# Two linear-attention directions paired on the PE array, and background modulation steps moved forward

## The chip, the cores and the metric

The kernel runs on one core of one Trainium2 chip. The time is device microseconds of one execution, from launch to the last result; the figure given for a kernel is the median of several executions. Engines are named as in the profile: PE is TensorE (matmuls), PEld its weight loads, DVE is VectorE, ACT is ScalarE, POOL is GpSimd, SP is SyncE, which here issues nearly all DMAs.

## The reference, cut to what matters

Two blocks of two layers each run over 256 latent tokens and 256 context tokens of width 1024, all in float32. The first block's layers compute windowed attention, a Fourier mix and a short convolution, gated and merged. Every layer is modulated: shift, scale and gate come from a small vector times a 1024 x 3072 matrix.

```python
def layer(x, ctx, c, c_ctx, w_mod, b_mod, ...):
    shift, scale, gate = jnp.split(jax.nn.silu(c) @ w_mod + b_mod, 3, axis=-1)
    hx = rmsnorm(x, g_pre) * (1 + scale[:, None]) + shift[:, None]
    ...
    x_new = x + gate[:, None] * rmsnorm(y, g_post)
```

The second block has nine modulation vectors per layer (`ada_w`), feed-forward stages, one even mixer and one odd mixer. The odd mixer is a gated linear attention with four heads, in chunks of 64 tokens, run forwards and backwards; the two results are added:

```python
def step(smat, inp):                       # one chunk of one direction
    ...
    o = a @ vc + qe @ smat                 # output of this chunk
    kd = kc * jnp.exp(bl - bcum)
    smat = jnp.exp(bl)[..., None] * smat + kd.T @ vc      # state for the next
    return smat, o
yx = yx_f + jnp.flip(yx_b, axis=1)
```

## The kernel before, in words

Weights come as chunks of 256 columns (1 MB) through `wload`, are split by ACT and DVE into a high and a low half (`wchunk`, L183 and L184), and each projection takes three one-pass products per 128 x 128 tile (`mm3`, L193 to L195). A raw chunk lies in one of three buffers during the first block: two of the pool `wraw` (tag `wr`) and one of `rx` (tag `xr`), handed out in turn. The split halves have two buffers each. A scheduler orders each engine's instructions at build time, by priority in program order and by a model of times; where a helper `row` is used, its products are issued one after the other in the order given.

**First block.** `fb_layer` runs for layer 0 and layer 1. While its projections run, a `hook` after each column tile of 128 does one step of the windowed attention and then `self.bg(HB)`: `HB` = 1 step from the queue `self.bgq` of background generators, taken in order. A generator that is at its end is dropped and the next one gives the step. Layer 0 has 16 such hooks. The queue holds `bga` (the modulation columns 2048 to 3072 of layer 0, 4 steps), `bgb` (the modulation of layer 1, 12 steps), `load_T` of the second block's context (3 steps: two with eight transposes each, L543, and copies, L545; one with the squares and sums of a norm's statistics) and `bgc` (modulation columns 0 to 3072 of the second block, 12 steps). A modulation step (`mods_pe`) loads 1 MB through the same `wload` (L319) and multiplies it (L322). `load_T` takes its raw tile from `wraw` and holds it until its second step. Its statistics (`Stat`) hold one buffer of tag `sq` (of three) and one of tag `sqa` (of two) until `c2stat.finish()` late in layer 1. After the hooks of layer 0 comes `drain_until(bgb)`, which steps the queue until `bgb` has left it. Then come the output projection (`twice`, six chunk loads), residual and norm, and layer 1, whose column tiles also do steps.

**Odd mixer.** A `plan` says which parts of the linear attention run in which hook of the value and gate projections. `begin` makes the state from the context, `advance(h, step)` does one chunk of both directions of head `h`: direction 0 takes chunk `step`, direction 1 chunk `3 - step`, so that they always use opposite halves of 64 rows. For each direction in turn it issues the output product (L1646: all 128 rows, 64 columns, into one half of the partitions), takes a bank `wk` of PSUM (the pool has three), issues the state product (L1649: 64 rows, 128 columns) and lets DVE update the state (L1651). The last of the four steps has no state product. Hooks 7, 8, 13 and 14 of the plan advance two heads with state products one after the other.

Of the kernel before, what the change touches and what calls it, by code (L numbers as in the profile page):

```python
# [10 lines left out]
ALU = mybir.AluOpType  # L11
# [34 lines left out]
C2A = 0  # L46
# [12 lines left out]
HB = 1  # L59
# [63 lines left out]
class Kern:  # L123
# [428 lines left out]
    def first_block(self):  # L552
        nc, I, tc = self.nc, self.I, self.tc
        V = self.vseg
        st = [self.Stat(self), self.Stat(self)]
        self.rope_tables(self.cp)
        with self.rawpool(RI):
            for _ in self.load_T(I["x"][0], self.X, st[0], self.wload):
                pass
            for i, _ in enumerate(self.mods_pe(I["w_mod"][0, :, 0:2048], 2048, self.m1[0][:, :, 0:16], V["bmod"][:, 0:16],  # L560
                                               self.cst, PM)):
                if i == 0:
                    self.late[0]()
                elif i == 3:
                    rbx = st[0].finish(alloc=self.sc)
                elif i == RL:
                    self.late[1]()
        st[0] = rbx
        bga = self.mods_pe(I["w_mod"][0, :, 2048:3072], 1024, self.m1[0][:, :, 16:24], V["bmod"][:, 16:24], self.cst)
        bgb = self.mods_pe(I["w_mod"][1], 3072, self.m1[1], V["bmod"][:, 24:48], self.cst)  # L570

        def ada():
            cst = self.set_cst(32)
            yield from self.mods_pe(I["ada_w_2"][0, :, 0:3072], 3072, self.m2[0][:, :, 0:24], V["adab0"][:, 0:24], cst)
        bgc = ada()
        self.c2stat = self.Stat(self)
        self.bgq = [bga, bgb, self.load_T(I["ctx_2"][0], self.C2, self.c2stat, act=C2A), bgc]
        with self.rawpool(RB), tc.tile_pool(name="fb", bufs=1, reuse_waits="tile") as self.fb:
            self.fb_layer(0, st, bga, bgb, self.fb_AB(0))
            if self.dbg != "fb0":  # L580
                self.fb_layer(1, self.nstat, None, bgc, self.nextAB)

# [6 lines left out]
    def fb_layer(self, l, stats, bga, bgb, AB):  # L589
        nc, I, tc = self.nc, self.I, self.tc  # L590
# [65 lines left out]
        def q_proj(c, korder=False, hook=None):  # L656
            self.proj(headchunk(0, c), c01, xn, qsegs, lambda i, ps: ev_q(i, ps, c), korder=korder, hook=hook, alloc=None if upd else self.facc)
# [57 lines left out]
        def attend():  # L715
            last = None
            for t in range(4):
                pso = None
                for si in range(nseg):
                    for i in range(2):  # L720
                        E = scores(t, si, i)
                        if last is not None:
                            values(*last)
                        if pso is None:
                            pso = self.wk()
                        last = (t, si, i, E, pso)
                        yield
            values(*last)
            yield

        att_gen = attend()

        def hook():
            next(att_gen, None)
            self.bg(HB)

        gf = [f1(f"gf{t}", TW) for t in range(2)]
        uf = [f1(f"uf{t}", TW) for t in range(2)]
# [55 lines left out]
        if l == 0:  # L794
# [4 lines left out]
            pss = [[self.facc() for _ in c01] for _ in first]  # L799
            for v, seg in enumerate(SEGS):  # L800
                if v == 1:
                    self.norm_seg(1, stats[1], A, B, PX)
                for j, ch in enumerate(first):
                    for i, cf in enumerate(c01):
# [3 lines left out]
                        if v == 1:  # L808
                            (ev_q if j else ev_kv)(i, pss[j][i])
            self.late[2]()  # L810
            q_proj(1, hook=hook)
        else:

# [8 lines left out]
            fourier()  # L822
            self.proj(self.wcols(w, 512), c01, xn, SEGS, ev_kv, hook=bgs(LB[3]))
            hook()
            self.proj(self.wcols(w, 2304), c01, xn, qsegs, ev_cc, hook=hook)
        if l == 0:
# [14 lines left out]
        h = self.xn  # L841
# [639 lines left out]
    def odd_mixer(self, stats):  # L1481
        nc, I, tc = self.nc, self.I, self.tc
# [6 lines left out]
        mm = nc.tensor.matmul  # L1489
        with self.rawpool(RO), tc.tile_pool(name="od", bufs=1, reuse_waits="tile") as od:  # L1490
# [9 lines left out]
            vt = od.tile([P, 4, D], F32, name="vt")  # L1500
# [3 lines left out]
            kT, qT, gs, kds, ats = {}, {}, {}, {}, {}  # L1504
# [122 lines left out]
            S, po, osbs = {}, {}, {}  # L1627
            vh = lambda h: slice(h * 256, (h + 1) * 256)
# [11 lines left out]
                    mm(po[h][i], ats[h][:, i], vt[:, i, vh(h)], start=(i == 0), stop=False)  # L1640

            def advance(h, step):
                for d in range(2):
                    c = 3 - step if d else step
                    i, r = c // 2, slice(64 * (c % 2), 64 * (c % 2) + 64)
                    mm(po[h][i][r], gs[h, d][0][:, c * 64:(c + 1) * 64], S[h, d], start=False, stop=(step == 3))  # L1646
                    if step < 3:
                        ps = self.wk()
                        mm(ps[:, 0:256], kds[h, d][r, i], vt[r, i, vh(h)], start=True, stop=True)  # L1649
                        s2 = od.tile([P, 256], F32, name="S", tag="S", bufs=6)  # L1650
                        nc.vector.scalar_tensor_tensor(s2, S[h, d], gs[h, d][4][:, c:c + 1], ps[:, 0:256], ALU.mult, ALU.add)  # L1651
                        S[h, d] = s2

            def norm(h):
# [12 lines left out]
            def gate(h):  # L1667
# [15 lines left out]
                4: [(turn, 1), (gates, 2)],  # L1683
                5: [(begin, 0, self.sc), (intra, 1), (decays, 2)],
                6: [(advance, 0, 0), (turn, 2), (begin, 1, self.sc), (gates, 3)],
                7: [(advance, 0, 1), (advance, 1, 0), (intra, 2), (decays, 3)],
                8: [(advance, 0, 2), (advance, 1, 1), (turn, 3)],
                9: [(advance, 0, 3), (advance, 1, 2), (intra, 3)],
                10: [(norm, 0), (advance, 1, 3)],
# [70 lines left out]
```

## Time and profile before

| | |
|---|---|
| median of 3 runs | 2285.04 us (2280.15 to 2288.1) |
| profiled execution | 2283.41 us |
| its span, first to last instruction | 2281.2 us |
| PE busy | 2207.0 us (97%) |
| DVE busy | 1540.7 us (68%) |
| ACT busy | 891.0 us (39%) |
| DMA | 327.27 MB, mean 143 GB/s |

Matmuls are pipelined, so "busy" counts from start to modelled end and overlaps between neighbours; the pace is read from one start to the next. A note such as `[2.07 <-ACT wh L177]` at the end of a row says that the engine was idle 2.07 us before it, and which instruction released it.

### The profile page before, as it was taken

To read this page: it belongs to the slowest core of one execution; us is meant where nothing else is said; L and a number is where in the kernel's file an instruction comes from. 1 tells how busy PE (TensorE), PEld (TensorE's weight loads), DVE (VectorE), ACT (ScalarE), POOL (GpSimd) and SP (SyncE) were. 2 spreads that over 40 slices of the span, in tenths; PEclk is the share of its full clock that TensorE was granted. 3 is DMA by queue.
4 is the path that set the end of the run, shared out by engine and by line. 5 is a ranking of instruction groups with operands and counts; after the bars stand their busy time and mean duration, and the time that the engine had idled before them with its cause. 6 is when DMAs were issued, how large, how long until landed. Compare 5 with 4: busy or idle time off the path is not lost.

```text
span 2281.2 us, 33404 instructions
## 1 busy us (share of the span) xinstructions
PE 2207.0 (97%) x13271; PEld 1882.1 (83%) x13271; DVE 1540.7 (68%) x3348; ACT 891.0 (39%) x1645; POOL 50.0 (2%) x113
## 2 busy tenths in 40 slices
PE   6999889999999999999999999999999999998998
PEld 4777786898888899877988888898888897778998
DVE  4644577786999876667769833469769475556555
ACT  3533555653222245444432221342222245534444
POOL 1000000000000000000000000000000010000000
PEclk8999999999999999999999999999999999999999
DMA  8334445644566432112436423245557242124553
GB/s 301 130 135 155 132 144 208 189 160 160 194 207 203 139 115 93 56 38 75 135 98 217 154 87 111 83 153 185 166 178 255 93 139 75 56 85 144 183 183 129
DMA packets 299179, 327.27 MB, mean 143 GB/s; under 512 B 9260, under 2 KB 290916, under 8 KB 295952
## 3 DMA queue, kind: packets, MB, share of 16 engines
q1 hardware_dynamic: 295968, 321.16, 43.7%
q8 instruction: 104, 1.70, 0.3%
q10 hardware_dynamic: 1952, 2.29, 0.3%
q0 software_dynamic: 1104, 1.70, 0.2%
q14 instruction: 51, 0.42, 0.1%
HBM read 324.07 MB, written 1.05 MB: 143 GB/s over the span
## 4 chain that ended last, share of the span: by engine, by line
PE 49%; issue 41%; DVE 5%; ACT 2%; DMA 2%; POOL 1%; SPq 0%; POOLq 0%; DVEq 0%; ACTq 0%
PE acc L193 9%; PE acc L194 9%; PE acc L195 9%; PE sc L193 3%; PE sc L194 3%; PE sc L195 3%; DVE wl L184 2%; PE acc L322 1%; PE acc L1090 1%; PE acc L1092 1%; PE acc L1091 1%; PE wk L704 1%; PE sc L1401 1%; ACT wh L183 1%; PE wk L1344 1%
## 5 line engine op out<-in xcount | busy, mean ns | idle before, releaser
L193 PE MATMUL acc<-xh,wh 128*128 128x256 f32 (+1 forms) x1792 | 611.5, 343 | 11.2 <-DVE qs L654 5.2
L195 PE MATMUL acc<-xh,wl 128*128 128x256 f32 (+1 forms) x1792 | 606.7, 339 | 5.9 <-DVE wl L184 5.9
L194 PE MATMUL acc<-xl,wh 128*128 128x256 f32 (+1 forms) x1792 | 606.8, 339 | 1.8 <-DVE xl L426 1.7
L183 ACT CAST wh<-wr 128x1024 fp32r<-128x1024 f32 (+1 forms) x394 | 385.9, 1024 | 542.6 <-PE acc L194 256.0
L184 DVE TENSOR_TENSOR wl<-wr,wh 128x1024 fp32r<-128x1024 f32 (+1 forms) x394 | 454.7, 1190 | 162.4 <-ACT wh L183 160.4
L193 PEld LDWEIGHTS acc<-xh,wh 128*128 128x128 f32 x1792 | 342.2, 192 | 69.7 <-issue 24.3
L195 PEld LDWEIGHTS acc<-xh,wl 128*128 128x128 f32 x1792 | 342.8, 191 | 42.8 <-DVE wl L184 6.5
L194 PEld LDWEIGHTS acc<-xl,wh 128*128 128x128 f32 x1792 | 343.2, 192 | 40.7 <-issue 5.0
L293 DVE SCALAR_TENSOR_TENSOR macc<-mraw,vec,macc 128x256 f32<-128x256 f32 x728 | 309.2, 477 | 2.4
L193 PE MATMUL sc<-xh,wh 128*128 128x256 f32 (+1 forms) x816 | 271.4, 333 | 6.3 <-ACT xh L425 3.5
L194 PE MATMUL sc<-xl,wh 128*128 128x256 f32 (+1 forms) x816 | 270.2, 332 | 0.9 <-DVE xl L426 0.9
L195 PE MATMUL sc<-xh,wl 128*128 128x256 f32 (+1 forms) x816 | 270.7, 332 | 0.0
L193 PEld LDWEIGHTS sc<-xh,wh 128*128 128x128 f32 x816 | 155.5, 191 | 22.0 <-ACT xh L425 4.4
L194 PEld LDWEIGHTS sc<-xl,wh 128*128 128x128 f32 x816 | 155.1, 190 | 15.4 <-DVE xl L426 1.3
L195 PEld LDWEIGHTS sc<-xh,wl 128*128 128x128 f32 x816 | 155.4, 190 | 14.1
L193 PE MATMUL acc<-hh,wh 128*128 128x256 f32 (+1 forms) x494 | 164.1, 332 | 0.0
L195 PE MATMUL acc<-hh,wl 128*128 128x256 f32 (+1 forms) x494 | 163.9, 332 | 0.0
L194 PE MATMUL acc<-hl,wh 128*128 128x256 f32 (+1 forms) x494 | 163.8, 332 | 0.0
L1022 ACT CAST hh<-hf 128x512 fp32r<-128x512 f32 (+1 forms) x92 | 50.1, 548 | 211.6 <-DVE hf L1017 211.6
L193 PE MATMUL sc<-hh,wh 128*128 128x256 f32 (+1 forms) x354 | 117.6, 332 | 0.0
L195 PE MATMUL sc<-hh,wl 128*128 128x256 f32 (+1 forms) x354 | 117.4, 332 | 0.0
L194 PE MATMUL sc<-hl,wh 128*128 128x256 f32 (+1 forms) x354 | 117.2, 331 | 0.0
(401 smaller groups left out, 2927.3 us busy)
## 6 DMA issues: line engine op xcount, KB each, us to landing
wr<-in_ffn_w_in_dram SPq DMA_DIRECT2D x92, 1024.0 KB, 5.1
mraw<-in_ada_w_dram SPq DMA_DIRECT2D x60, 1024.0 KB, 5.1
wr<-in_ffn_w_out_dram SPq DMA_DIRECT2D x32, 1024.0 KB, 5.3
wr<-in_ffn_w_out_dram SPq DMA_DIRECT2D x22, 768.0 KB, 4.5
xr<-in_w_mod_dram SPq DMA_DIRECT2D x14, 1024.0 KB, 7.4
wr<-in_even_w_in_dram SPq DMA_DIRECT2D x12, 1024.0 KB, 5.2
wr<-in_odd_w_in_dram SPq DMA_DIRECT2D x12, 1024.0 KB, 5.3
wr<-in_w_mod_dram SPq DMA_DIRECT2D x10, 1024.0 KB, 5.4
```

What stands on the lines that cost most here:

```text
L183: nc.scalar.copy(hi[:, a:b], raw[:, a:b])
L184: nc.vector.tensor_tensor(lo[:, a:b], raw[:, a:b], hi[:, a:b].bitcast(F32), ALU.subtract)
L193: mm(ps, wh, xh, start=start, stop=False)
L194: mm(ps, wh, xl, start=False, stop=False)
L195: mm(ps, wl, xh, start=False, stop=stop)
L293: nc.vector.scalar_tensor_tensor(a, raw[:, k], cs[:, v * 8 + k:v * 8 + k + 1], a, ALU.mult, ALU.add)
L322: ins = nc.tensor.matmul(ps[32 * j:32 * j + 32, 0:cw], vec[:, k], raw[:, k - k0, j * cw:(j + 1) * cw], start=(k == 0), stop=(k == KT - 1))
L704: nc.tensor.transpose(p2[:, j * P:(j + 1) * P], E[:, hh, j * P:(j + 1) * P], self.ident)
L1022: nc.scalar.copy(h[0][:, sl], hf)
L1090: mm(o, xn[k][0][:, s], hi[:, k, :], start=(k == 0), stop=False)
L1091: mm(o, xn[k][0][:, s], lo[:, k, :], start=False, stop=False)
L1092: mm(o, xn[k][1][:, s], hi[:, k, :], start=False, stop=(k == KT - 1))
```

## The change

It makes two edits. First, `advance` issues the output products of both directions as one row (direction 1 first), then both state products as one row, each with a PSUM bank of its own, and then the two updates. Second, `bgc` is appended to the background queue only after layer 0, and the first six hooks of layer 0 do two background steps each instead of one.

```diff
-        self.bgq = [bga, bgb, self.load_T(I["ctx_2"][0], self.C2, self.c2stat, act=C2A), bgc]
+        self.bgq = [bga, bgb, self.load_T(I["ctx_2"][0], self.C2, self.c2stat, act=C2A)]
         with self.rawpool(RB), tc.tile_pool(name="fb", bufs=1, reuse_waits="tile") as self.fb:
             self.fb_layer(0, st, bga, bgb, self.fb_AB(0))
+            self.bgq.append(bgc)
...
+        early = [6 if l == 0 else 0]
+
         def hook():
+
             next(att_gen, None)
-            self.bg(HB)
+            self.bg(HB + (early[0] > 0))
+            early[0] -= 1
...
             def advance(h, step):
+
+                at_ = []
                 for d in range(2):
                     c = 3 - step if d else step
-                    i, r = c // 2, slice(64 * (c % 2), 64 * (c % 2) + 64)
-                    mm(po[h][i][r], gs[h, d][0][:, c * 64:(c + 1) * 64], S[h, d], start=False, stop=(step == 3))
-                    if step < 3:
-                        ps = self.wk()
-                        mm(ps[:, 0:256], kds[h, d][r, i], vt[r, i, vh(h)], start=True, stop=True)
+                    at_.append((d, c, c // 2, slice(64 * (c % 2), 64 * (c % 2) + 64)))
+                pss = [self.wk()[:, 0:256] for _ in range(2)] if step < 3 else []
+
+                self.row([((po[h][i][r], gs[h, d][0][:, c * 64:(c + 1) * 64], S[h, d]), dict(start=False, stop=(step == 3)))
+                          for d, c, i, r in at_[::-1]])
+                if step < 3:
+                    self.row([((pss[d], kds[h, d][r, i], vt[r, i, vh(h)]), dict(start=True, stop=True)) for d, c, i, r in at_])
+                    for d, c, i, r in at_:
                         s2 = od.tile([P, 256], F32, name="S", tag="S", bufs=6)
-                        nc.vector.scalar_tensor_tensor(s2, S[h, d], gs[h, d][4][:, c:c + 1], ps[:, 0:256], ALU.mult, ALU.add)
+                        nc.vector.scalar_tensor_tensor(s2, S[h, d], gs[h, d][4][:, c:c + 1], pss[d], ALU.mult, ALU.add)
                         S[h, d] = s2
```

## Rows read from the trace of the kernel before

**Rows 1.** The page, part 1: busy us of each engine, instructions.
```profile
PE 2207.0 (97%) x13271; PEld 1882.1 (83%) x13271; DVE 1540.7 (68%) x3348; ACT 891.0 (39%) x1645; POOL 50.0 (2%) x113
```

**Rows 2.** Stretches: length, PE, PEld, DVE, ACT, POOL busy, granted clock, DMA.
```profile
230.00:241.00 11.00, 7.14 (x56) 4.54 (x55) 6.21 (x20) 6.58 (x15) 0.00 (x0) 0.78 0.35 99
...
251.00:268.00 17.00, 15.03 (x112) 13.87 (x111) 11.83 (x23) 11.04 (x23) 0.40 (x8) 1.00 0.46 125
...
300.00:312.00 12.00, 6.43 (x37) 6.02 (x36) 10.26 (x21) 5.54 (x13) 0.00 (x0) 0.72 0.30 98
...
340.00:375.00 35.00, 29.84 (x154) 22.26 (x150) 25.08 (x56) 17.26 (x36) 0.00 (x0) 0.90 0.66 238
...
2020.00:2040.00 20.00, 20.00 (x105) 12.28 (x104) 9.80 (x16) 6.45 (x13) 0.00 (x0) 1.00 0.17 53
```

**Rows 3.** Timeline of PE: start, us, line, operation; one step of one head.
```profile
1972.76 0.65 PE L1646 MATMUL sc<-S,qe 128*64 128x256 f32 x2
1973.34 0.70 PE L1649 MATMUL wk<-vt,kdt 64*128 64x256 f32 x2
1973.96 0.65 PE L1646 MATMUL sc<-S,qe 128*64 128x256 f32 x2
...
1975.16 0.65 PE L1646 MATMUL sc<-S,qe 128*64 128x256 f32 x2
```

**Rows 4.** Timeline of PE: a head's last step, both directions, and what follows.
```profile
2002.95 0.65 PE L1646 MATMUL sc<-S,qe 128*64 128x256 f32 x4
2003.54 0.38 PE L193 MATMUL acc<-xh,wh 128*128 128x256 f32 x1
```

**Rows 5.** Timeline of PE: attention scores, one full product, then two half-height ones.
```profile
113.61 0.40 PE L204 MATMUL sc<-kh,qs 128*128 128x512 f32 x1
113.93 0.50 PE L204 MATMUL sc<-klo,qs 64*128 64x512 f32 x2
114.37 0.66 PE L704 MATMUL wk<-ident,E 128*128 128x128 f32 x4
```

**Rows 6.** Line L1651, the state updates: min/median/max ns, first and last start.
```profile
L1651 DVE SCALAR_TENSOR_TENSOR S<-S,ebl,wk x24: 455/479/482, 1962.4 to 2040.5; 128x256 f32<-128x256 f32 x24
```

**Rows 7.** Timeline of DVE: a chunk's split, between state updates.
```profile
2022.27 2.35 DVE L184 TENSOR_TENSOR wl<-wr,wh 128x1024 fp32r<-128x1024 f32 x2
```

**Rows 8.** Timeline of SP's queue: DMA issues of the first block.
```profile
67.86 0.37 SPq L168 DMA_DIRECT2D wr<-in_w_in_dram  x1
...
213.28 0.37 SPq L538 DMA_DIRECT2D wr<-in_ctx_dram  x1
...
232.11 1.00 SPq L168 DMA_DIRECT2D wr<-in_w_in_dram  x2
...
290.24 1.91 SPq L168 DMA_DIRECT2D wr<-in_w_out_dram  x3
...
325.60 0.34 SPq L319 DMA_DIRECT2D wr<-in_ada_w_dram  x1
```

**Rows 9.** Timeline of PE: first block, with idle time before and its releaser.
```profile
80.84 0.47 PE L193 MATMUL acc<-xh,wh 128*128 128x512 f32 x1 [3.38 <-DVE qs L654]
...
236.93 1.12 PE L543 MATMUL wk<-ident,wr 128*128 128x128 f32 x4
240.12 0.79 PE L193 MATMUL acc<-xh,wh 128*128 128x512 f32 x1 [2.07 <-ACT wh L177]
...
307.20 0.58 PE L195 MATMUL acc<-xh,wl 128*128 128x256 f32 x1 [5.03 <-DVE wl L184]
...
324.53 1.03 PE L543 MATMUL wk<-ident,wr 128*128 128x128 f32 x8
...
354.97 1.25 PE L322 MATMUL acc<-wr,cst 128*32 128x512 f32 x8 [2.15 <-DMA wr<-in_ada_w_dram]
```

**Rows 10.** The page, part 6: DMA issues, KB each, median us to landing.
```profile
xr<-in_w_mod_dram SPq DMA_DIRECT2D x14, 1024.0 KB, 7.4
```

## Prediction

> **What bounds the kernel now.** I read the page's table of engines first: TensorE is busy 97% of the span [rows 1], so time goes only where TensorE's own work shrinks, or where one of its few gaps closes. Then the table by stretches, to see which of these the two edits can touch [rows 2]. There the reader is to see that in a stretch of linear attention (2020 to 2040) TensorE is busy for all 20 us while VectorE is at 9.8: work taken from TensorE there moves the end. And that around the border of the first block's two layers TensorE has holes: 11 - 7.14 = 3.9 us in 230 to 241, 17 - 15.03 = 2.0 in 251 to 268, 12 - 6.43 = 5.6 in 300 to 312, 35 - 29.84 = 5.2 in 340 to 375. In these the granted clock falls to 0.72 to 0.90 (0.78 in the first), a mix of the 2.4 and 1.2 GHz levels, and it falls after idle time. Third came TensorE's order of instructions, fourth SyncE's DMA issues.
>
> **Linear attention, the part whose size can be worked out.** One step of one head is now four products in the order output, state, output, state, and takes 1975.16 - 1972.76 = 2.40 us [rows 3]: 0.58 for an output product (1972.76 to 1973.34), 0.62 for a state product (to 1973.96), twice. The change puts the two output products next to each other; they write opposite halves of the partitions, so they use opposite column halves of the array. The last step of a head already has them so, since it has no state product: four passes, two products, take 2003.54 - 2002.95 = 0.59 [rows 4], as much as one alone. So an output pair falls from 1.16 to 0.59.
>
> The state pair (64 rows each, opposite row halves) does not occur in the old trace. Its bounds: 0.62 if the second is free, 1.24 if it overlaps not at all. The nearest row is the pair of half-height score products: both take 114.37 - 113.93 = 0.44, where one full product of the same columns takes 113.93 - 113.61 = 0.32 [rows 5], so the second adds 0.12. Those are one-pass products and the state products have two passes, so I add 0.18, between 0.12 and 0.24, and take 0.80. A step is then 0.59 + 0.80 = 1.39 and saves 1.0; there are 12 steps with state products (4 heads, 3 steps each; 24 updates in [rows 6]), which gives 12 us. With the bounds it is 12 x 0.57 = 7 to 12 x 1.19 = 14. The fourth steps gain nothing.
>
> The Trainium skill (TensorE: Matmul & The Clock Gate, Measured speedup vs the span model) puts a further tile in a pack at some 4 ns. By that the state pair would cost 0.62 and the edit give 14 us; the row of score pairs shows 120 ns instead, and the measurement decides.
>
> What it costs: the state row takes two work banks of PSUM at once, of three, and frees them only by VectorE's updates of 0.48 each [rows 6]. Queued behind a waiting row on TensorE are the other head's state row, then the next projection. In four hooks two heads advance one after the other: the second state row needs the first update done, which is about 0.1 + 0.48 after the first row, while its own output pair fills 0.59. That just closes. Where a weight split of 2.35 for two halves stands between updates, as once here [rows 7], it doesn't. Bounds 0 and 4 x 2.35 = 9.4; I take 1, since the old order of VectorE shows one such place in four and a projection can be placed ahead of the row. Sum: 12 - 1 = **11 us gained**.
>
> **The background steps, work that is only moved.** Layer 0 has 16 hooks. So far they run exactly the 4 + 12 steps of the two modulations, and the call that drains the queue then runs the first step of loading the second context. Its raw tile is one of only three raw weight buffers (two "wr", one "xr"), and its second half is transposed only in layer 1. After the change hooks 1 to 6 run two steps, hooks 7 to 10 one, hooks 11 to 13 the whole context load, hooks 14 to 16 none; layer 1 begins straight with the next modulation, two hooks earlier, 12 steps instead of 14. TensorE's instructions stay the same in number. What changes is who holds buffers when.
>
> That the context's tile is what blocks is seen in SyncE's queue [rows 8]: it is loaded at 213.28, its last transposes stand at 324.53 [rows 9], and the next load into its slot goes out at 325.60, right after. For 112 us one of three buffers is gone. Stage by stage:
> - *Layer 0's end.* The last gate projection waits 2.07 us at 240.12 [rows 9] for a chunk whose load went out only at 232.11, just after the last modulation step. With that step six hooks earlier, the load goes out a projection earlier, and the projection can also fill the other 1.8 us of hole beside the last attention steps. Against it: the context's first transposes (1.12 and as many before it, some 1.7 us with overlap [rows 9]) lose this hole as cover and go into full stretches. The clock, 0.78 over these 11 us, comes back in part, worth 1.4 of (1 - 0.78) x 11 = 2.4. Sum -3.9 - 1.4 + 1.7 = -3.6.
> - *Output projection.* At 307.20 TensorE has waited 5.03 us for the low half of the last output chunk [rows 9]; its load went out at 290.24, and VectorE ran the norm of x in between. With a third buffer it can load some 15 us earlier and be split before the norm. The clock of 0.72 in that stretch [rows 2] is worth 1 to 2 more, the hole in 251 to 268 about 1. But VectorE is nearly full here (10.3 of 12), so I count -6 of the possible 9.
> - *Layer 1.* Two modulation loads are waited for, the longer 2.15 us [rows 9]. They start earlier and with one buffer more, but at the layer's start three projections now also carry two steps each. Of 5.2 us I count -3.4.
> - *Early hooks.* The next chunk's load (67.86 [rows 8]) now shares the ring with four modulation loads per projection instead of two, and goes out only after hook 1's products, at 80.84 - 3.38 = 77.5 [rows 9]. A load of that ring lands some 7 us later [rows 10], and a split takes 2.35 [rows 7], so it is ready at about 87; I estimate that it is needed at about 90, after 5.5 us of the running column and the two hooks' attention work. On the other side the hole of 3.38 us itself, a wait for VectorE's eviction, gets room when that split moves away. Bounds -3 and +4, taken as 0.
>
> Sum **13 us gained**, bounds 3 to 20.
>
> **Sum.** The profiled execution took 2283.4 (span 2281.2 and 2.2 around it), 1.6 under the median of the runs shown. 2283.4 - 11 - 13 = 2259.4, rounded to **2260**.
>
> **Rivals.**
> 1. *The border stays bound by VectorE.* The statistics of the second context (one of three "sq" buffers, one of two "sqa") are now held through the whole layer border, so the residual's own statistics have less room and its norm comes later. For it: VectorE is at 10.3 of 12 in 300 to 312. Against: the statistics there are used nearly one after the other. The border then gives 4 instead of 13: 2283.4 - 11 - 4 = 2268.
> 2. *The state pair does not overlap, or waits for banks.* Every step saves 0.57 and the stalls are 2: 7 - 2 = 5. Then 2283.4 - 5 - 13 = 2265. The Trainium skill (TensorEngine Tiling, Gotcha 1: PSUM Pressure) warns of this side, that row tiles need separate banks; each state product has its own bank here.
> 3. *All holes close and the state pair is free.* 20 + 13 gives 2250.
> 4. *Slower: the weight ring starves early.* If each chunk's load is queued behind the second hook's modulation products, landing (7.4 us [rows 10]) and split (2.35) are bare in three projections: 3 x 10 us and about 1.4 us each for the fallen clock, +34. It decides when a chunk goes out less than some 10 us before its projection. Against: by the reckoning above it goes out 12 us before. With the 24 gained: 2283.4 + 34 - 24 = 2293.
> 5. *The move does not do what it says*: the loads stay blocked by something else and the early cost is 3, so the border gives 0: 2283.4 - 11 + 3 = 2275.
>
> **How the numbers follow.** About 0.3%, or 7 us, is what a measurement of this kernel tells from no change. Chances: forecast 0.48 (2254 to 2266 by itself), rival 1 0.18, rival 2 0.11, rival 3 0.11, rival 4 0.05, rival 5 0.07. All but rival 4 and half of rival 5 lie under 2278: faster 0.9, same 0.05, slower 0.05. The range leaves out rival 4 and the fringes: 2250 to 2275.
>
> **What would show it.** In the new trace a step of linear attention should last 1.3 to 1.5 us, with the two state products starting within 0.2 of each other; more than 1.8 means no overlap. TensorE idle in front of state rows with VectorE as releaser means rival 2. The waits at 240 and 307 should be gone, no context transposes should stand in layer 1, and the last output chunk's load should go out 10 us or more ahead of its old place. A wait for a weight chunk or a modulation load between 85 and 125 means rival 4. I am wrong if TensorE's gaps between 230 and 375 sum to about as much as before.

## The result and the profile after

The changed kernel takes 2258.17 us (median of 4 runs, 2255.24 to 2259.77), the kernel before, beside it, 2284.68: a ratio of 0.9889, 95% interval 0.9875 to 0.9903. Forecast were 2260 and 2250 to 2275. The profiled execution's span is 2255.6 us, 25.6 less than before.

Where they went is read first from one event that both kernels have at the same place of their work: the second block's first modulation load.

```profile
443.99 0.44 SPq L286 DMA_DIRECT2D mraw<-in_ada_w_dram  x1
```

That was SyncE's queue in the kernel before; in the changed kernel it goes out 13.3 us earlier:

```profile
430.68 0.44 SPq L286 DMA_DIRECT2D mraw<-in_ada_w_dram  x1
```

The first block has gained 13.3. Where in the block is shown by the norm of x that opens layer 1, which both kernels have as well (L413 spreads its factor over the partitions). Before, then changed:

```profile
298.06 0.68 PE L413 MATMUL wk<-dg,ones 128*128 128x128 f32 x4 [0.75 <-DVE dg L403]
```

```profile
298.31 0.68 PE L413 MATMUL wk<-dg,ones 128*128 128x128 f32 x4
```

Here the changed kernel is still 0.25 behind. From this norm to the load it takes 430.68 - 298.31 = 132.4 us where the kernel before took 145.9: the whole gain of the first block arises there. Then the stretches; columns as in [rows 2]. Of the kernel before, early hooks, border of the layers, and linear attention from its first output product to its last:

```profile
74.00:130.00 56.00, 52.62 (x341) 37.30 (x340) 32.15 (x84) 28.78 (x62) 0.00 (x0) 1.00 0.48 169
...
230.00:375.00 145.00, 126.89 (x860) 108.91 (x858) 102.08 (x244) 75.18 (x165) 3.56 (x12) 0.93 0.51 158
...
1958.77:2042.90 84.13, 83.84 (x505) 62.28 (x504) 45.17 (x102) 34.29 (x71) 2.38 (x5) 1.00 0.18 56
```

And of the changed kernel, the same three, and between them those that answer to [rows 2]:

```profile
74.00:130.00 56.00, 55.92 (x341) 36.07 (x339) 28.63 (x75) 23.42 (x52) 0.00 (x0) 1.00 0.64 226
...
230.00:375.00 145.00, 135.93 (x947) 115.49 (x946) 101.05 (x249) 74.24 (x159) 3.56 (x12) 0.96 0.49 158
...
230.00:241.00 11.00, 11.00 (x59) 8.61 (x58) 4.87 (x11) 3.89 (x9) 0.00 (x0) 1.00 0.20 46
251.00:268.00 17.00, 15.20 (x106) 15.20 (x107) 11.05 (x25) 9.72 (x24) 0.40 (x8) 0.80 0.46 126
300.00:312.00 12.00, 12.00 (x103) 12.00 (x102) 11.16 (x21) 8.44 (x19) 0.00 (x0) 1.00 0.27 90
...
1943.26:2017.30 74.04, 70.85 (x504) 57.16 (x504) 43.57 (x97) 34.18 (x71) 2.25 (x5) 1.00 0.18 59
```

The reader is to see three things. TensorE's idle time between 230 and 375 has halved, 18.1 to 9.1, and in the early hooks it went from 3.4 to 0.1. The linear attention is 84.13 - 74.04 = 10.1 shorter: TensorE's work there fell by 83.84 - 70.85 = 13.0, but its idle time rose from 0.3 to 3.2. The 25.6 are thus 13.3 + 10.1 and 2.2 elsewhere, of which 1.6 belong to the clock and to neither edit (last section).

One step of linear attention now, TensorE's timeline (L201 is the first product of a row, L204 the others; each product has two passes):

```profile
1957.25 0.43 PE L201 MATMUL sc<-S,qe 128*64 128x256 f32 x1
1957.26 0.43 PE L204 MATMUL sc<-S,qe 128*64 128x256 f32 x1
1957.52 0.38 PE L201 MATMUL sc<-S,qe 128*64 128x256 f32 x1
1957.52 0.38 PE L204 MATMUL sc<-S,qe 128*64 128x256 f32 x1
...
1957.83 0.48 PE L201 MATMUL wk<-vt,kdt 64*128 64x256 f32 x1
1957.84 0.48 PE L204 MATMUL wk<-vt,kdt 64*128 64x256 f32 x1
...
1958.46 0.43 PE L201 MATMUL sc<-S,qe 128*64 128x256 f32 x1
```

The output pair takes 0.58, the state pair 0.63, the step 1.21 where [rows 3] showed 2.40. The second product of each pair starts 0.01 after the first, and its second pass with the second pass of the first (1957.52).

The changed kernel's larger waits of TensorE, first block, then linear attention:

```profile
250.25 0.39 PE L193 MATMUL acc<-xh,wh 128*128 128x256 f32 x1 [2.16 <-ACT xh L444]
252.80 0.58 PE L194 MATMUL acc<-xl,wh 128*128 128x256 f32 x1 [1.82 <-DVE xl L445]
...
1945.38 0.30 PE L1605 MATMUL wk<-ident,tk 128*128 128x128 f32 x1 [0.83 <-DVE tk L1597]
...
1947.48 0.33 PE L1605 MATMUL wk<-ident,tk 128*128 128x128 f32 x1 [0.44 <-DVE S L1661]
...
1968.37 0.70 PE L201 MATMUL wk<-vt,kdt 64*128 64x256 f32 x2
...
1972.38 0.70 PE L204 MATMUL wk<-vt,kdt 64*128 64x256 f32 x2 [1.82 <-DVE S L1661]
```

The waits of [rows 9] at 80.84 (3.38), 240.12, 307.20 and 354.97 are gone. New are two behind each other at 250, for the split halves of the gated tiles, two smaller ones in layer 1 (1.66 at 344.34 for the Fourier stage, 1.00 at 346.48 for a head's split), and in the linear attention one state row torn apart: its first product runs at 1968.37, its second at 1972.38, since its bank is freed only by a state update. VectorE's timeline says why that is late: two weight splits and a head's decays (seven rows of L1595 to L1598, 0.42 each) stand before it.

```profile
1967.11 1.22 DVE L184 TENSOR_TENSOR wl<-wr,wh 128x1024 fp32r<-128x1024 f32 x1
...
1968.92 1.22 DVE L184 TENSOR_TENSOR wl<-wr,wh 128x1024 fp32r<-128x1024 f32 x1
...
1971.84 1.75 DVE L1661 SCALAR_TENSOR_TENSOR S<-S,ebl,wk 128x256 f32<-128x256 f32 x4
```

SyncE's queue shows the loads that answer to [rows 8]: the context's, a gate chunk's (x2), and two chunks of the output projection, the last of them.

```profile
175.58 0.52 SPq L538 DMA_DIRECT2D wr<-in_ctx_dram  x1
...
204.37 1.00 SPq L168 DMA_DIRECT2D wr<-in_w_in_dram  x2
...
251.84 14.70 SPq L168 DMA_DIRECT2D wr<-in_w_out_dram  x6
```

The gate chunk goes out 27.7 us before its old place (232.11), the last output chunk by 266.5 instead of 290.24. The context's last transposes (L543) start at 204.1: its tile now holds a buffer for some 29 us and not for 112, and no longer across the border.

### The profile page after: what moved, and what is told of

Read it like the earlier page. It is cut to its first block, busy times and chain, and to the rows that moved or that the text cites. A ratio compares the mean times of both kernels' runs of the same rounds, so it can differ in the third digit from the quotient of the medians.

```text
span 2255.6 us, 33407 instructions
## 1 busy us (share of the span) xinstructions
PE 2190.3 (97%) x13271; PEld 1875.7 (83%) x13271; DVE 1540.3 (68%) x3348; ACT 890.4 (39%) x1645; POOL 49.9 (2%) x113
## 4 chain that ended last, share of the span: by engine, by line
PE 49%; issue 41%; DVE 6%; ACT 2%; DMA 1%; POOL 1%; SPq 0%; DVEq 0%; POOLq 0%; ACTq 0%
PE acc L193 9%; PE acc L194 9%; PE acc L195 8%; PE sc L193 3%; PE sc L194 3%; PE sc L195 3%; DVE wl L184 2%; PE acc L322 1%; PE acc L1097 1%; PE acc L1095 1%; PE acc L1096 1%; PE wk L705 1%; PE sc L1406 1%; PE wk L1349 1%; PE sc L204 1%
```

## The experiments

**The two edits alone.** First the linear attention's edit, with the background steps as before:

```diff
-        self.bgq = [bga, bgb, self.load_T(I["ctx_2"][0], self.C2, self.c2stat, act=C2A)]
+        self.bgq = [bga, bgb, self.load_T(I["ctx_2"][0], self.C2, self.c2stat, act=C2A), bgc]
-            self.bgq.append(bgc)
...
-            self.bg(HB + (early[0] > 0))
+            self.bg(HB)
```

> Only the linear attention's edit; the background steps stay as in the kernel before. Theory: the rows save about 1.2 us in each of the 12 steps with state products and lose about 3 in new stalls, 11 in all as predicted: 2285 - 11 = 2274, ratio 0.995. In the trace the first block should stand within 0.5 us of the kernel before up to 450 us, and the whole difference should arise in the odd mixer. Rival (the two edits need each other, because the scheduler weighs both): less than 8 or more than 14 gained, 2277 or 2271.

Ratio 0.9954 (0.994 to 0.9968), 2271.85 us beside 2281.44 before. The linear attention takes what it takes in the changed kernel (74.04):

```profile
1955.50:2029.60 74.10, 70.88 (x505) 57.14 (x504) 43.60 (x97) 34.24 (x71) 2.29 (x5) 1.00 0.18 59
```

The expected sameness up to 450 us did not quite come: 2.4 us of difference arose there, in unchanged code. So single traces differ by a couple of us, and the terms below are read from stretches, not from the ends of spans.

Then the background's edit, with `advance` as before:

```diff
-                self.row([((po[h][i][r], gs[h, d][0][:, c * 64:(c + 1) * 64], S[h, d]), dict(start=False, stop=(step == 3)))
-                          for d, c, i, r in at_[::-1]])
...
+                    mm(po[h][i][r], gs[h, d][0][:, c * 64:(c + 1) * 64], S[h, d], start=False, stop=(step == 3))
+                    if step < 3:
+                        ps = self.wk()
+                        mm(ps[:, 0:256], kds[h, d][r, i], vt[r, i, vh(h)], start=True, stop=True)
```

> Only the background's edit; the linear attention stays as in the kernel before. Theory: 13 us gained, all of it before 450 us, 2285 - 13 = 2272, ratio 0.994; the sum of this gain and that of the rows alone is the whole gain of 26.5 within 2 us. Rival (the two edits need each other): the sum misses 26.5 by more than 3 us.

Ratio 0.9936 (0.9922 to 0.995), 2267.82. 0.9954 x 0.9936 = 0.9890, the changed kernel's ratio within 0.0001, where each interval is 0.0014 either way. In microseconds the two gains were 9.6 and 13.6, together 23.2 and so 3.3 short of the 26.5; by the mark set beforehand that speaks for the rival. But the kernel before took 2281.44 beside these two and 2284.68 beside the changed kernel, which is as much. The traces decide: with the background's edit alone the load of L286 goes out at 432.12 (441.61 with the rows alone), and the linear attention takes 83.8 us, from 1945.76 to 2029.59 (74.1 with the rows alone). Each edit works in its own stretch, and neither needs the other.

**Which part of the background's edit.** Three double hooks instead of six; then six, but with the third modulation in the queue from the start:

```diff
-        early = [6 if l == 0 else 0]
+        early = [3 if l == 0 else 0]
```

> The changed kernel with three double hooks instead of six: the 19 steps of layer 0 then end exactly with hook 16, the context is loaded in hooks 14 to 16, none of its steps is left for layer 1. Theory (what counted was the context's tile held across the border): nearly the whole gain stays, 2257 to 2261. Rival (what counts is that the last three hooks carry no steps, so that the last chunks of the layer are loaded early): the wait for a gate chunk at the end of layer 0 comes back, 2263 to 2266.

```diff
-        self.bgq = [bga, bgb, self.load_T(I["ctx_2"][0], self.C2, self.c2stat, act=C2A)]
+        self.bgq = [bga, bgb, self.load_T(I["ctx_2"][0], self.C2, self.c2stat, act=C2A), bgc]
-            self.bgq.append(bgc)
```

> The changed kernel with the third modulation left in the queue from the start: the last three hooks of layer 0 then run its first three steps, and layer 1 has nine of its steps left instead of twelve. Theory (held tile): no buffer is held for long, and what layer 0 pays layer 1 gets back, 2256 to 2260. Rival (the last hooks must be free of steps): the end of layer 0 waits for its gate chunk again, 2262 to 2266.

Ratios 0.9885 (0.9869 to 0.99) and 0.9889 (0.9873 to 0.9906): neither differs measurably from the changed kernel. Within some 3 us, the width of these intervals to either side, it does not matter that the last hooks are free of steps, nor when `bgc` joins the queue.

**The held buffer itself.** One and two double hooks differ in one step only, the one that frees the context's raw tile: with one it falls into layer 1, with two into the last hook of layer 0.

```diff
-        early = [6 if l == 0 else 0]
+        early = [1 if l == 0 else 0]
```

> The changed kernel with one double hook instead of six: 17 steps in layer 0, so the context's first step runs in its last hook and its second, which frees the raw buffer, only in layer 1. Theory (held buffer): the buffer is held across the border as in the kernel before, the output projection waits some 5 us again, 2264 to 2270 (the rows' gain alone is 10). Rival (the double steps matter by their number or by the free last hooks): a smooth loss, about the same here as with two double hooks.

```diff
-        early = [6 if l == 0 else 0]
+        early = [2 if l == 0 else 0]
```

> The changed kernel with two double hooks: 18 steps in layer 0, so the context's second step runs in its last hook and the raw buffer is free before the border; only its statistics step is left for layer 1. Theory (held buffer): nearly as fast as with three or six double hooks, 2255 to 2260, and at least 5 us faster than with one double hook. Rival: no more than 2 us faster than with one.

Measured: 2269.09 with one (0.9935, 0.9921 to 0.9948) and 2256.71 with two (0.9883, 0.9869 to 0.9896). 12.4 us hang on that step. With one double hook, the context's transposes (line L543: count, min/median/max ns, first and last start), the wait in the output projection, the border:

```profile
L543 PE MATMUL wk<-ident,wr x32: 272/283/473, 8.6 to 326.4; 128*128 128x128 f32 x32
```

```profile
308.83 0.58 PE L195 MATMUL acc<-xh,wl 128*128 128x256 f32 x1 [5.04 <-DVE wl L184]
```

```profile
230.00:375.00 145.00, 129.21 (x858) 111.51 (x856) 101.12 (x241) 74.57 (x164) 3.58 (x12) 0.93 0.51 156
```

With two:

```profile
L543 PE MATMUL wk<-ident,wr x32: 272/374/473, 8.1 to 236.5; 128*128 128x128 f32 x32
```

```profile
230.00:375.00 145.00, 136.62 (x970) 116.02 (x968) 109.78 (x269) 81.87 (x177) 3.68 (x12) 0.98 0.54 172
```

While the last transposes stand at 326 the 5 us wait of [rows 9] is back (5.04 for 5.03) and TensorE idles 15.8 of the 145 us; with the last transposes at 236.5 it idles 8.4. SyncE issues the last output chunk's load at 291.69 with one double hook, and by 264.7 with two.

The same from the other side: the kernel before, nothing doubled, only the context's load moved behind the third modulation.

```diff
-        self.bgq = [bga, bgb, self.load_T(I["ctx_2"][0], self.C2, self.c2stat, act=C2A), bgc]
+        self.bgq = [bga, bgb, bgc, self.load_T(I["ctx_2"][0], self.C2, self.c2stat, act=C2A)]
```

> The kernel before with one change: the context's load stands last in the background queue, behind the third modulation, so that its raw tile is taken and given back within layer 1 and no buffer is held across the border. No hook does two steps, the linear attention is as before. Theory (the held buffer is the cause): the 5 us wait in the output projection goes and the border gives 6 to 11 of the 13 us, 2271 to 2276. Rival (the double steps are the cause, since they end layer 0's steps early): within 3 us of the kernel before, 2279 to 2284, with the 5 us wait still there.

2274.09, ratio 0.9953 (0.994 to 0.9965), 10.2 us gained by order alone. No wait of 5 us is left at its border (230 to 375), and 10.4 us of idle time stand where the kernel before had 18.1.

From the norm of x (L413) to the load of L286 the kernels fall into two groups:

| kernel | context's tile at the border | norm of x | load | between |
|---|---|---|---|---|
| before | held | 298.06 | 443.99 | 145.9 |
| rows alone | held | 297.33 | 441.61 | 144.3 |
| one double hook | held | 299.68 | 444.03 | 144.4 |
| two double hooks | given back | 296.72 | 427.36 | 130.6 |
| three double hooks | given back | 296.48 | 428.44 | 132.0 |
| the change (six) | given back | 298.31 | 430.68 | 132.4 |
| background alone (six) | given back | 298.75 | 432.12 | 133.4 |
| six, third modulation queued at once | given back | 300.17 | 431.56 | 131.4 |
| context last | not yet loaded | 299.37 | 432.62 | 133.3 |

Held or not makes 11 to 15 us, whatever the order of the other steps. The norm of x itself comes between 296.5 and 300.2 in all of them, in no order that follows the double hooks. Double hooks are one way to give the buffer back early, not the cause of the gain. No run gave the context's tile a buffer of its own, so what else moves with its step (eight transposes, some 1 us of TensorE) is not parted from it.

**Which pair gives what.** The state products kept apart by the output pair (`b` is direction 1, `a` direction 0):

```diff
+                o = lambda d, c, i, r: ((po[h][i][r], gs[h, d][0][:, c * 64:(c + 1) * 64], S[h, d]), dict(start=False, stop=(step == 3)))
+                s = lambda d, c, i, r: ((pss[d], kds[h, d][r, i], vt[r, i, vh(h)]), dict(start=True, stop=True))
+                b, a = at_[::-1]
+                if step == 3:
+                    self.row([o(*b), o(*a)])
+                else:
+                    self.row([s(*a), o(*b), o(*a), s(*b)])
```

> The changed kernel, but in each step with state products the two output products alone stand next to each other; the state products stand before and behind them, so they can't share the array. Theory from the traces (a pair of either kind costs what one product costs: 0.58 and 0.63): a step of 0.58 + 2 x 0.62 = 1.82 instead of 1.21, so the stretch of the linear attention is 12 x 0.61 = 7 us longer than in the changed kernel, less 1 to 3 of the stalls that the faster step has; 2262 to 2265. By the prediction's sizes (state pair 0.80, gain 0.44 a step) it would lose only 5: 2263. Rival (the state pair gives nothing in the end, because its banks come back late): 2258 to 2260.

And the output products kept apart by the state pair, as an edit of that kernel:

```diff
-                    self.row([s(*a), o(*b), o(*a), s(*b)])
+                    self.row([o(*b), s(*a), s(*b), o(*a)])
```

> The changed kernel, but the two state products alone stand next to each other, the output products of the step before and behind them. Theory (pairs are as cheap as one product): a step of 2 x 0.58 + 0.63 = 1.79, so the stretch is 12 x 0.58 = 7 us longer than in the changed kernel, less 1 to 3 of its stalls, 2262 to 2265; start of one state product to that of the other 0.01 us. Rival: the output pair gives nothing, 2258.

Outputs paired: 2261.26, ratio 0.9897 (0.9882 to 0.9913). States paired: 2260.12, 0.9894 (0.9879 to 0.991). Both lie just under the 2262 to 2265 expected, and as times neither is clear of the changed kernel; the traces decide. A step with the output pair alone:

```profile
1957.34 0.70 PE L201 MATMUL wk<-vt,kdt 64*128 64x256 f32 x2
1957.97 0.65 PE L204 MATMUL sc<-S,qe 128*64 128x256 f32 x4
1958.55 0.70 PE L204 MATMUL wk<-vt,kdt 64*128 64x256 f32 x2
1959.09 0.59 PE L201 MATMUL wk<-vt,kdt 64*128 64x256 f32 x2
```

and with the state pair alone:

```profile
1955.55 0.65 PE L201 MATMUL sc<-S,qe 128*64 128x256 f32 x2
1956.12 0.70 PE L204 MATMUL wk<-vt,kdt 64*128 64x256 f32 x4
1956.75 0.65 PE L204 MATMUL sc<-S,qe 128*64 128x256 f32 x2
1957.24 0.59 PE L201 MATMUL sc<-S,qe 128*64 128x256 f32 x2
```

They take 1959.09 - 1957.34 = 1.75 and 1957.24 - 1955.55 = 1.69, against 2.40 and 1.21: a pair alone saves 0.65 or 0.71 of a step, both together 1.19. The products left apart follow their like of the next step after 0.54 (state) or 0.49 (output) instead of 0.62 and 0.58; why, the runs do not show. The stretch of linear attention, in the same order:

```profile
1944.00:2021.80 77.80, 76.19 (x501) 59.94 (x502) 43.56 (x99) 34.06 (x70) 2.38 (x5) 1.00 0.18 56
```

```profile
1941.60:2019.50 77.90, 76.73 (x505) 59.46 (x504) 43.55 (x97) 34.22 (x71) 2.24 (x5) 1.00 0.17 55
```

Either pair alone gains 6.3 or 6.2 of 84.1; both together 10.1, not 12.5. Of what is missing, 1.8 is TensorE's work (it fell by 7.7 or 7.1, and by 13.0), and 0.7 is idle time, which grows with TensorE's pace: 0.3, then 1.6 or 1.2, then 3.2. Expected losses of 7 less 1 to 3 of stalls came out as 3.8 and 3.9 in the stretch: the stalls were as said (1.6 and 2.0 less), but a pair taken apart cost only 5.3 or 5.9 of work.

**Banks or VectorE.** One product of each state row in a bank of the projections' pool:

```diff
-                pss = [self.wk()[:, 0:256] for _ in range(2)] if step < 3 else []
+                pss = [self.wk()[:, 0:256], self.acc()[:, 0:256]] if step < 3 else []
```

> The changed kernel with one product of each state row in a bank of the projections' pool (three banks) instead of both in the pool of three work banks. Theory (the 1.8 us in front of a state row and smaller ones are a shortage of work banks, rival 2 of the prediction): that wait goes, 1 to 2 us gained, 2256 to 2257. Rival (the wait is VectorE, whose updates stand behind decays and splits): the bank is free earlier, but the next step or the projection waits for the same update, 2257 to 2260.

Ratio 0.9871 (0.9853 to 0.989), 2255.59: nearer to the theory's 2256 to 2257 than to the rival's 2257 to 2260, but not distinguishable from the changed kernel; the linear attention took 75.0. The trace speaks for the rival. The torn row is whole, and the wait has gone to the transposes behind it:

```profile
1966.63 0.30 PE L1605 MATMUL wk<-ident,tk 128*128 128x128 f32 x1 [0.15 <-PE acc L204]
1968.02 0.33 PE L1606 MATMUL wk<-ident,scx 128*128 128x128 f32 x1 [1.08 <-DVE scx L1598]
1969.87 0.38 PE L1605 MATMUL wk<-ident,tk 128*128 128x128 f32 x1 [0.84 <-DVE S L1661]
```

0.15 + 1.08 + 0.84 = 2.07 for the 1.82 of before: the bank was only where the wait for VectorE became visible.

State updates ahead of VectorE's other work, with three double hooks:

```diff
+                        with tc.high_priority(offset=WP):
-                        nc.vector.scalar_tensor_tensor(s2, S[h, d], gs[h, d][4][:, c:c + 1], pss[d], ALU.mult, ALU.add)
+                            nc.vector.scalar_tensor_tensor(s2, S[h, d], gs[h, d][4][:, c:c + 1], pss[d], ALU.mult, ALU.add)
```

> The kernel with three double hooks, and the state updates of the linear attention given priority over VectorE's weight splits and decays, so that the banks of a state row come free at once. Theory (the rows' stalls are banks that wait for updates queued behind the decays): of the idle 1.8, 0.8 and 0.4 us that TensorE has there 1.5 to 3 go, 2253 to 2255, ratio 0.987 to 0.9878. Rival (the same work waits for the decays themselves, so the wait only moves to the turn behind it): no gain, 2256, or a loss of 1 to 2 where a weight split comes later.

Ratio 0.9879 (0.9865 to 0.9892), no gain over the same kernel without it (0.9885). In its trace the first updates of that hook still stood behind two splits and three decays, and the wait before the torn row only shrank to 1.64, at 1970.37. So priority did not do what I wanted of it, and the run says little about what earlier updates would bring.

The last run asks for VectorE's results later. With two double hooks, each `turn` was planned a hook later (and the first `intra` kept behind its `turn`):

```diff
-                2: [(turn, 0), (gates, 1)],
-                3: [(intra, 0), (decays, 1)],
-                4: [(turn, 1), (gates, 2)],
-                5: [(begin, 0, self.sc), (intra, 1), (decays, 2)],
+                2: [(gates, 1)],
+                3: [(turn, 0), (intra, 0), (decays, 1)],
+                4: [(gates, 2)],
+                5: [(begin, 0, self.sc), (turn, 1), (intra, 1), (decays, 2)],
...
```

> The kernel with two double hooks, and the transposes of each head's decayed keys planned one hook later (the products inside a chunk of the first head too), so that TensorE reaches them after VectorE has made them. Theory (TensorE's remaining idle time in the linear attention is VectorE's decays, read just in time): of the waits of 2.1, 2.7, 0.8, 0.4 and 1.8 us in front of transposes and of a state row some 3 to 6 go, 2251 to 2254, ratio 0.986 to 0.9872. Rival (VectorE itself is the bound there, so the waits come back elsewhere): 2256 to 2258.

2249.49, ratio 0.9846 (0.9831 to 0.9861): faster than both kernels. Of the five waits of 2.1, 2.7, 0.8, 0.4 and 1.8 us that the kernel with two double hooks has, 0.16 is left at a transpose, and two longer ones before products:

```profile
1936.96 1.13 PE L1639 MATMUL wk<-vt,kdt 128*128 128x256 f32 x4 [1.72 <-DVE S L1661]
```

```profile
1961.35 0.70 PE L204 MATMUL wk<-vt,kdt 64*128 64x256 f32 x2 [1.32 <-DVE S L1661]
```

The two longest that went are no stalls of the faster step. They stand ahead of the first output product, and the kernel before has them too:

```profile
1922.22 0.33 PE L1600 MATMUL wk<-ident,tk 128*128 128x128 f32 x1 [2.10 <-DVE tk L1592]
...
1939.24 0.33 PE L1600 MATMUL wk<-ident,tk 128*128 128x128 f32 x1 [2.72 <-DVE tk L1592]
```

In the linear attention itself, from the first output product on, the kernel with later turns still idles 75.90 - 72.60 = 3.3 us, as the changed kernel does (3.2):

```profile
1932.90:2008.80 75.90, 72.60 (x505) 58.66 (x504) 43.46 (x97) 34.21 (x71) 2.18 (x5) 0.98 0.18 57
```

So later turns closed waits that were there before the change; the stalls that came with the faster step no run here has removed. The waits fell by 4.7 in all and the time by 7, below the 2251 to 2254 expected. With the two long waits the fallen clock went too: the stretch ahead of the first output product has 0.92 with two double hooks (1900 to 1941.5) and 1.00 with later turns (1892 to 1932.9).

## Why the prediction was right, step by step

**Linear attention: 11 forecast, 10.1 in the trace, by two terms that were off against each other.** The output pair came as said, 0.58 for 0.59. The state pair was mis-sized: 0.63 for the 0.80 that I took from the pairs of scores. The Trainium skill (TensorE: Matmul & The Clock Gate, Measured speedup vs the span model), with its 4 ns for a further tile, was the better guide: the trace has 10 ns. Why the score pair costs 0.12 more than one product the runs do not show. So a step saves 1.19 and not 1.0; in eleven of the twelve rows, one being torn, that is 13.1, and TensorE's work fell by 13.0. The stalls were mis-sized the other way, 1 forecast, 3.2 - 0.3 = 2.9 measured. I had priced only updates that stand behind a weight split; one such place came, in one of the four hooks named, but half of what VectorE did there was a head's decays, and at 1945 and 1947 it was the transposes that caught up with them. The clause that failed is the one that looked only at banks for what is late next. Rival 2's first half fell (the pair overlaps fully); its second half was real, with VectorE rather than the banks as the cause.

**Background: 13 forecast, 13.3 in the trace, but not where the terms had it.** Up to the norm of x the terms of the early hooks and of layer 0's end promised 3.6 us; there the changed kernel was 0.25 behind, with two background steps more done (eight transposes and a statistics step, some 1 us of TensorE). From there on the other two terms had 9.4, and 13.6 were gained. The held buffer was the right mechanism; that its price came to 13 in all is luck, two errors off against each other.
- *Early hooks*, forecast 0: 52.62 became 55.92 busy of 56. The hole of 3.38 closed as its clause allowed, and its price was not due: no wait for a chunk or a modulation load stands between 85 and 125, although the chunk's load went out only at 79.27, later than the 77.5 I had reckoned with. Rival 4 fell. But the 3.3 can't all be put down to the edit: before 74 the changed kernel idles 1.0 more, and with early hooks left as they were the same hole took 3.4, 2.8 and 2.0 us (kernel before, rows alone, context last).
- *Layer 0's end*, forecast 3.6: 230 to 241 is full and its clock 1.00, as said. But 241 to 251, full before, now idles 2.2, 251 to 268 kept its idle time (2.0 before, 1.8 now), and its clock, which [rows 2] has at 1.00 and not among the fallen ones as the prediction says, fell to 0.80. The projection now arrives before ScalarE and VectorE have made its inputs (2.16 and 1.82). This next wait I had not named, and the 1 us that I counted for that stretch did not come.
- *Output projection*, forecast 6: the 5.03 wait is gone, 300 to 312 went from 6.43 to 12.00 busy and from 0.72 to 1.00 in clock. VectorE at 11.16 of 12 did not stop it. Rival 1 fell.
- *Layer 1*, forecast 3.4: the idle time of 340 to 375 went from 5.2 to 2.7, but 312 to 340, nearly full before (0.1), now idles 1.7. The 2.15 for a modulation load is gone; the Fourier stage and a head's split came up in its place (1.66 and 1.00).

Up to the load of L286 idle time fell by 11.4 in all (42.4 to 31.0), and TensorE's work, the same 2730 products, by 1.9 (401.6 to 399.7). I put the 1.9 down to the clock (0.93 to 0.96 over the border), which was not measured apart.

**The cause** that the sum rested on, the raw buffer held by the context's tile, is shown and not only argued: 12.4 us between one and two double hooks, 10.2 by the queue's order alone, and two groups of kernels 11 to 15 us apart between the same two events. Rival 5 fell with it. That double hooks were the means in the change is incidental: two do as well as six.

## What to carry to other kernels

When a ring of few buffers feeds the bound engine, look for the one tile that sits in it across a stage: its load and its last reader in the trace give the time it was held, and moving that one step can be worth more than faster products (here 12.4 us and 9.6). To see where a gain arises, take two events that every kernel has and compare the time between them; idle time in fixed windows mixes in work that has moved. Two products that use opposite halves of the array belong next to each other in the issue order; their price here was one product's, but the engine behind them must then keep the new pace, and what it has queued there, not only its banks, belongs in the sum. A gain of a pair and its stalls are separate terms: a good sum can hide that both were wrong.

## What the runs showed of the hardware

That the passes of two float32 products on opposite halves interleave, first passes 0.01 apart and second passes at most 0.01, I had not expected; I had let the second passes cost extra.

The clock did not answer to idle time alone. At the start of the odd mixer TensorE has the same two waits in both kernels, 0.73 and then 0.88 us. In the kernel before, the granted clock fell after them, from 1.00, the level of 2.4 GHz:

```profile
1880.73 0.50 PE L193 MATMUL acc<-xh,wh 128*128 128x512 f32 x1 [0.88 <-ACT xh L425]
```

```profile
1881.00:1884.00 3.00, 3.00 (x8) 2.11 (x8) 3.00 (x9) 2.09 (x6) 0.70 (x1) 0.58 0.03 5
```

In the changed kernel it did not:

```profile
1866.82 0.73 PE L193 MATMUL acc<-xh,wh 128*128 128x512 f32 x2 [0.88 <-ACT xh L425]
```

```profile
1867.00:1870.00 3.00, 3.00 (x13) 2.25 (x14) 3.00 (x9) 2.09 (x6) 0.79 (x1) 1.00 0.02 5
```

The same 120 products took 24.2 us there and 22.6 here. All fourteen kernels have these two waits. In the 3 us behind the second one the clock was 0.51 to 0.65 in five of them (the kernel before, background alone, two double hooks, updates first, outputs paired) and 1.00 in the other nine. What decides stays open; 1.6 us of a span's difference can come and go with it.
